# First sweep of a hybrid encoder layer: projection weights in another column order, with another row pitch, and small tiles at the end of their pool

## The chip, the core and the metric

The kernel runs on one core of one Trainium2 chip. The metric is the device time of one execution in microseconds (us), taken as the median of several runs. Beside the timed runs there is one profiled execution, whose page and trace give the start and the duration of every instruction. Engines are named as the profile does: PE (TensorE, matmul), PEld (its weight loads), DVE (VectorE), ACT (ScalarE), POOL (GpSimd), SP (the queue that issues most transfers).

## The reference

One encoder layer on x of shape (1, 2048, 1024), float32. One combined input projection feeds two mixers, whose outputs are joined, projected and added to the residual before a layer norm:

```python
h = x @ w_in
(g_q, g_k, g_v, g_gate, g_lr_f, g_lr_b,
 m_cq, m_ckv, m_kr, m_gate) = jnp.split(h, idx, axis=-1)
o_a = gla_branch(g_q, g_k, g_v, g_gate, g_lr_f, g_lr_b, wg2_f, bg_f, wg2_b, bg_b, gla_norm_g)
o_b = mla_branch(m_cq, m_ckv, m_kr, m_gate, positions, q_norm_g, w_uq, kv_norm_g, w_ukv)
mixed = jnp.concatenate([o_a, o_b], axis=-1) @ w_out
x = layer_norm(DEEPNORM_ALPHA * x + mixed, ln_g[layer], ln_b[layer])
```

Mixer A is gated linear attention with 4 heads (key width 64, value width 128), computed in chunks, as a forward and a backward scan that are summed. Mixer B is latent attention with 4 heads and a dense softmax over all 2048 keys.

## The kernel before

Every matmul operand is a float32 number split into a high and a low part (both of type float32r), and every product is three matmuls into one PSUM tile: high x high, high x low, low x high (`mm3`, lines 418 to 422; in the profile L420, L421 and L422). In `mm3(out, ah, al, bh, bl)` a is the stationary operand, which is loaded anew for each matmul, and b the moving one.

The work is done in four stages. The first sweep (`sweep_a`, some 22 to 350 us after the weights have come) walks the 16 chunks of 128 rows of x from the last to the first. For a chunk it computes the projections for mixer A's low-rank decay, q, k and v: the transposed chunk of x (tiles `xah` and `xal`, 8 blocks of 128 x 128) is stationary, and the weight rows `wah{k}` and `wal{k}` (k = 0 to 7, one tile of 128 x 1056 for each part) move, in three column groups of 288, 384 and 384 columns: `A_GROUPS = ((0, 288), (288, 384), (672, 384))`. Column group 0 holds the low-rank columns and q, group 1 k and the first head of v, group 2 the other three heads of v. The products of a group land in one PSUM tile `ipa` (`products`, lines 735 to 755). Between them stand, in a fixed order per chunk, the small products of the scan: transposes `qT`, `kT`, `kt`, `lrT`, the decay product `z`, the scores inside a chunk `Ap` (`ga_intra`), the output `Op` (`ga_av`) and the state update `Up` (`ga_state`). A fourth group `ipg` computes a gate of 512 columns with other weights (`wgh`, `wgl`).

The second sweep (`sweep_c`, to some 600 us) does the projections and the small products of mixer B (`ipm`, `pz`, `pq`, `pqr`) and combines the scan's state (`Sf`, `SU`, `MMb`, `qhb`, `qlb`, product `Ob`); then come the attention (`pS`, `o`) and the output projection (`po`, `pmb`, `px`).

The order of instructions on each engine is written out (`STEPS_A`, `ORDER_A` and tables of places), so that an edit of a tile's address alone does not reorder the first sweep. Tiles live in pools, which place them one behind the other in a partition. The pool `wa` holds the first sweep's weights and fixed tiles; behind it stand, first, the staging tiles `was` for the weights as they come from memory and later the pool `g1` with the working tiles of a chunk. So the size of a small tile early in `wa` shifts all that comes after it. The tiles of the second sweep are laid over this region, and their first writers wait until the earlier tiles that they overlap have had their last reader. SP issues its transfers in program order: a transfer that waits holds back those behind it.

The lines that the change touches:

```python
wa = [[wp.tile([P, NA], F32R, name=f"wa{p}{k}") for p in "hl"] for k in range(NK)]
...
self.mm3(pt[:, :n], xh[:, k, 0], xl[:, k, 0], wh[:, c0:c0 + n], wl[:, c0:c0 + n],
         start=(k == 0), stop=(k == NK - 1))
```

Of the kernel before, what the change touches and what calls it, by code (L numbers as in the profile page):

```python
# [9 lines left out]
F32 = mybir.dt.float32  # L10
F32R = mybir.dt.float32r
# [7 lines left out]
P = 128  # L19
S = 2048  # L20
D = 1024
NK = D // P
NCH = S // P
H = 4
NA = 1056
W_PIECES = ((2, 2, 2, 2), (2, 2, 2, 2), (2, 2, 2, 2))
A_GROUPS = ((0, 288), (288, 384), (672, 384))
QB = 512
NQB = S // QB
NKT = S // P  # L30
# [114 lines left out]
    xh=(-0.19, -0.054),  # L145
# [27 lines left out]
    xl=(-0.154, 0.109),  # L173
# [51 lines left out]
    xh=(-0.3, 1.403),  # L225
# [27 lines left out]
    xl=(1.031, 1.013),  # L253
# [37 lines left out]
    xh=(-0.262, -0.109),  # L291
# [27 lines left out]
    xl=(-0.244, 0.038),  # L319
# [36 lines left out]
class K:  # L356
# [254 lines left out]
    def sweep_a(self):  # L611
        tc, nc, ins, cp = self.tc, self.nc, self.ins, self.cp
        with ExitStack() as ctx:
            wp = ctx.enter_context(tc.tile_pool(name="wa", bufs=1, reuse_waits="tile"))
            xp, ip, tr, gp = self.xab, self.ip, self.tr, self.gp


            wa = [[wp.tile([P, NA], F32R, name=f"wa{p}{k}") for p in "hl"] for k in range(NK)]
            mask = wp.tile([P, P], I32, name="mask")
            rmask = wp.tile([P, H, P], F32, name="rmask")  # L620
            wgm = wp.tile([98, 1], F32, name="wgm")
            wg = wp.tile([98, H, P], F32R, name="wg")
            lrs = [wp.tile([P, 98], F32R, name=f"lr{i}") for i in range(2)]
            qbh = [wp.tile([P, H, 2, P], F32R, name=f"qbh{i}") for i in range(1)]
            qbl = [wp.tile([P, H, 2, P], F32R, name=f"qbl{i}") for i in range(1)]
            Sb = wp.tile([P, H, P], F32, name="Sb")
            pos_i = wp.tile([P, NCH], I32, name="pos_i")
            pos_f = wp.tile([P, NCH], F32, name="pos_f")
            invf = wp.tile([P, 32], F32, name="invf")
            hpi = wp.tile([P, 1], F32, name="hpi")  # L630
            self.cos = self.keep.tile([P, NCH, 32], F32, tag="rm", name="cos")
            self.sin = self.keep.tile([P, NCH, 2, 32], F32, tag="acc", name="sin")
            nc.scalar.preload_act_table_set(EXP_LN)
            for t in lrs:
                nc.vector.memset(t[:, 96:98].bitcast(F32), 1.0)
            for t in qbh + qbl:
                nc.gpsimd.memset(t.bitcast(F32), 0.0)
            nc.vector.memset(Sb, 0.0)

            with tc.tile_pool(name="sta", bufs=1, reuse_waits="tile") as sta:  # L640
                xf = self.load_x(NCH - 1, "xa", 1, 2)
                xcur = self.split_x(xp, xf, NCH - 1, "xa", "dve", 2)
                wgf = sta.tile([98, H * P], F32, name="wgf")
                wgh = sta.tile([98, H * P], F32R, name="wgh")
                W, wdone = wa, []
                for g, (c0, n) in enumerate(A_GROUPS):
                    k = 0
                    for m in W_PIECES[g]:
                        st = sta.tile([P, m, n], F32, name=f"was{g}_{k}")
                        nc.sync.dma_start(st, ins["wA"][k:k + m, :, c0:c0 + n].rearrange("k p n -> p k n"))  # L650
                        for e in range(m):
                            wh, wl = wa[k + e]
                            ops = (self.hi(wh[:, c0:c0 + n], st[:, e]),
                                   self.lo(wl[:, c0:c0 + n], st[:, e], wh[:, c0:c0 + n]))
                        k += m
                        wdone.append(ops)
                    if g == 0:
                        nc.sync.dma_start(self.ident, ins["ident"])
                        nc.sync.dma_start(wgf, ins["wg"])
                        nc.sync.dma_start(wgm, ins["wgm"])  # L660
                xnext = self.split_x(xp, self.load_x(NCH - 2, "xa", 1, 2), NCH - 2, "xa", "dve", 2)
                nc.sync.dma_start(rmask, ins["rmask"])
                nc.sync.dma_start(mask, ins["mask"])
                self.hi(wgh, wgf)
                nc.vector.scalar_tensor_tensor(wg.rearrange("p h d -> p (h d)"), wgh.bitcast(F32), wgm[:, 0:1],
                                               wgf, ALU.mult, ALU.add)
            nc.sync.dma_start(pos_i, ins["pos"])
            nc.sync.dma_start(invf, ins["invf"])
            g1 = ctx.enter_context(tc.tile_pool(name="g1", bufs=1))

            cst = dict(qbh=qbh[0], qbl=qbl[0], Sb=Sb, mask=mask, rmask=rmask, wg=wg, g1=g1, tr=tr, gp=gp)
            rope = self.rope_angles(pos_i, pos_f, invf, hpi)
            ch = self.ch = [dict(cst, c=NCH - 1 - i, i=i, lr=lrs[i % 2]) for i in range(NCH)]
            self.wa = wa
            run = lambda n, i: [0 for _ in getattr(self, "ga_" + n)(ch[i])]
            ch[0]["x"], ch[1]["x"] = xcur, xnext

            def step(i, steps):

                def after(g, k):  # L680
                    for n, d in steps.get((g, k), ()):
                        run(n, i if d == "cur" else i - 1)
                for g in range(3):
                    for k in self.products(ch[i], g, after):
                        pass
                    after(g, NK - 1)
                if i and ch[i]["c"] not in LATE_GATES:
                    for k in self.gate_products(ch[i]["c"], *ch[i]["x"], ip):
                        after(3, k)
                    self.gate_end(ch[i]["c"], g1)  # L690

            self.first_lr = wdone[7][0]
            step(0, {(1, 7): [("lrT", "cur")]})
            run("bst", 0)
            self.wgr = [self.wgp.tile([P, 512], F32, tag="wg", name=f"wgr{k}") for k in range(NK)]
            for k, raw in enumerate(self.wgr):
                nc.sync.dma_start(raw, ins["wB"][k, :, 0:512])
            self.wgh = [self.wgp.tile([P, 512], F32R, tag="wg", name=f"wgh{k}") for k in range(NK)]
            gens, last = {}, {}
            for t in ORDER_A.split():  # L700
                n, i = t.split(".")
                if t not in gens:
                    gens[t] = getattr(self, "ga_" + n)(int(i) if n in ("wg", "ld", "x") else ch[int(i)])
                with self.in_order(last):
                    next(gens[t], None)
            for n, g in gens.items():
                assert not list(g), n
            for i in range(4, NCH):
                c = ch[i]["c"]
                if c > 0:  # L710
                    for f in (self.ga_ld, self.ga_x):
                        for _ in f(i + 1):
                            pass
                else:
                    self.xlate = [self.split_x(xp, self.load_x(NCH - 1, "xb"), NCH - 1, "xb")]
                    self.xraw = self.load_x(NCH - 2, "xb")
                step(i, STEPS_A)
                if i < 4 + 5:
                    with self.after(ch[i]["zdone"]):
                        next(rope)  # L720
                if i == 9:
                    self.rope_tables(hpi)
            i = NCH - 1
            run("q", i)
            run("k", i)
            run("av", i - 1)
            for k in self.gate_products(0, *ch[i]["x"], ip):
                if k == 5:
                    run("kt", i)
                    run("intra", i)  # L730
            self.gate_end(0, g1)
            run("state", i)
            run("av", i)

    def products(self, d, g, after=lambda g, k: None):

        nc, c, i, g1 = self.nc, d["c"], d["i"], d["g1"]
        c0, n = A_GROUPS[g]
        xh, xl = d["x"]
        if i == 0 and g == 2:  # L740
            pt = self.gp.tile([P, 1024], F32, tag="gp", name=f"ipa{c}_{g}")
# [1 line left out]
            pt = self.ip.tile([P, 512], F32, tag="ip", name=f"ipa{c}_{g}")  # L743
        d["pt", g] = pt
        for k in range(NK):
            wh, wl = self.wa[k]
            self.mm3(pt[:, :n], xh[:, k, 0], xl[:, k, 0], wh[:, c0:c0 + n], wl[:, c0:c0 + n],
                     start=(k == 0), stop=(k == NK - 1))
            if k < NK - 1:
                after(g, k)  # L750
            yield k
# [145 lines left out]
    def ga_sums(self, d):  # L897
# [7 lines left out]
        V.tensor_tensor_scan(f2(b)[64:128, ::-1], f2(rmask)[64:128, ::-1], f2(za)[64:128, ::-1],  # L905
                             0.0, ALU.mult, ALU.add)
        yield
        cl = d["cl"] = d["g1"].tile([P, 3, H], F32, tag="cl", name=f"cl{c}")
        V.tensor_copy(cl[0:64, 0], b[0:64, :, 63])
        V.tensor_copy(cl[64:128, 0], b[64:128, :, 64])  # L910
        V.tensor_copy(cl[0:64, 2], b[0:64, :, 127])
# [1100 lines left out]
```

## Time and profile before

| | before |
|---|---|
| median of 3 runs | 1317.59 us (1316.13 to 1318.52) |
| span of the profiled execution | 1311.9 us |
| median less that span (no separate time of the profiled execution is given) | 5.7 us |
| TensorE busy | 1288.3 us, 98% |
| VectorE, ScalarE, GpSimd busy | 958.5, 812.5, 784.6 us |
| mean granted TensorE clock | 0.998 |

In a row of a group the profile gives line, engine, operation, out<-in by the program's names (buffer numbers left out), the shapes, how often it occurs, then the busy time in us, the mean ns of one instruction, and the idle time of the engine just before them with what ended it. Matmuls are pipelined: the duration of one includes a part that overlaps the next one.

### The profile page before, as it was taken

How to read it: one execution, taken by the hardware profiler on the slowest of the kernel's cores; microseconds unless marked ns; L12 is line 12 of the kernel's file. 1: busy time of each engine (PE TensorE's matmuls, PEld its weight loads, DVE VectorE, ACT ScalarE, POOL GpSimd, SP SyncE). 2: the span in 40 equal slices, each digit the busy share in tenths (PEclk: the TensorE clock that was granted, in tenths of full speed). 3: DMA queues.
4: the chain of work that ended last, by engine and by line, in shares of the span. 5: the costliest groups of instructions: out<-in, count | busy, mean ns of one | idle time of the engine just before them, and what ended most of it. 6: DMA issues, size and time to landing. Idle time of an engine off the chain costs nothing.

```text
span 1311.9 us, 19981 instructions
## 1 busy us (share of the span) xinstructions
PE 1288.3 (98%) x7081; PEld 1129.9 (86%) x7081; DVE 958.5 (73%) x1712; ACT 812.5 (62%) x1339; POOL 784.6 (60%) x494
## 2 busy tenths in 40 slices
PE   7999999999999999999999999999999999999997
PEld 7999999999989999999788888888888887888786
DVE  7967684655675455554888888888888888468998
ACT  6765656555575656564687787888888888511110
POOL 0143333232457666671388888889999999844441
PEclk9999999999999999999999999999999999999999
DMA  8131313122475555565301111112223210366663
GB/s 283 61 100 53 93 53 92 49 76 71 147 245 173 197 194 177 201 202 177 121 1 41 41 42 41 41 57 59 63 66 102 51 41 9 121 208 174 210 195 121
DMA packets 107819, 145.81 MB, mean 111 GB/s; under 512 B 17250, under 2 KB 62694, under 8 KB 107720
## 3 DMA queue, kind: packets, MB, share of 16 engines
q1 hardware_dynamic: 99128, 142.41, 35.0%
q0 software_dynamic: 672, 2.10, 0.4%
q8 instruction: 56, 0.92, 0.3%
q10 hardware_dynamic: 7920, 0.03, 0.3%
q14 instruction: 43, 0.35, 0.2%
HBM read 94.14 MB, written 50.36 MB: 110 GB/s over the span
## 4 chain that ended last, share of the span: by engine, by line
PE 83%; DVE 4%; DMA 3%; ACT 2%; issue 2%; POOL 1%; SPq 1%; DVEq 0%; POOLq 0%; ACTq 0%
PE o L420 4%; PE o L421 4%; PE pS L1521 4%; PE pS L1524 4%; PE o L422 4%; PE pS L1523 4%; PE pS L1525 4%; PE pS L1522 4%; PE ipa L420 4%; PE ipa L422 4%; PE ipa L421 4%; PE pz L421 2%; PE pz L420 2%; PE pz L422 2%; PE ipg L420 2%; PE ipg L421 2%
## 5 line engine op out<-in xcount | busy, mean ns | idle before, releaser
L372 POOL TENSOR_TENSOR pl<-s,ph 128x1024 fp32r<-128x1024 f32 x128 | 306.9, 2412 | 66.7 <-ACT ph L366 61.5
L1543 DVE TENSOR_TENSOR rm<-pS,rm 128x512 f32<-128x512 f32 x210 | 144.8, 690 | 44.1 <-ACT s L1530 39.0
L1530 ACT ACTIVATE s<-pS 128x1024 f32<-128x1024 f32 x128 | 131.2, 1025 | 67.6 <-PE pS L1525 65.6
L1567 DVE TENSOR_TENSOR s<-s,mb 128x1024 f32<-128x1024 f32 x128 | 151.2, 1213 | 9.5 <-PE mb L1561 9.3
L1030 POOL TENSOR_TENSOR Us<-Us,cw 128x512 f32<-128x512 f32 x16 | 18.5, 1157 | 227.0 <-DVE Us L1028 175.2
L366 ACT ACTIVATE ph<-s 128x1024 fp32r<-128x1024 f32 x128 | 135.0, 1057 | 18.1 <-PE o L422 17.6
L1571 ACT ACTIVATE s<-s 128x1024 f32<-128x1024 f32 x128 | 131.4, 1050 | 13.8 <-DVE s L1567 13.7
L420 PE MATMUL ipa<-wah,xah 128*128 128x384 f32 (+1 forms) x384 | 130.6, 340 | 6.8 <-ACT wah L366 6.8
L422 PE MATMUL ipa<-wah,xal 128*128 128x384 f32 (+1 forms) x384 | 125.2, 326 | 0.0
L421 PE MATMUL ipa<-wal,xah 128*128 128x384 f32 (+1 forms) x384 | 125.0, 325 | 0.0
L1521 PE MATMUL pS<-qh,ckvT_h 128*128 128x512 f32 x256 | 103.7, 405 | 0.7 <-ACT s L1571 0.4
L420 PE MATMUL o<-ph,vh 128*128 128x512 f32 x256 | 102.6, 401 | 0.0
L422 PE MATMUL o<-ph,vl 128*128 128x512 f32 x256 | 101.3, 396 | 0.0
L1524 PE MATMUL pS<-rh,krs 128*128 128x512 f32 x256 | 101.2, 395 | 0.0
L421 PE MATMUL o<-pl,vh 128*128 128x512 f32 x256 | 101.1, 395 | 0.0
L1523 PE MATMUL pS<-qh,ckvT_l 128*128 128x512 f32 x256 | 100.9, 394 | 0.0
L1525 PE MATMUL pS<-rl,krs 128*128 128x512 f32 x256 | 100.7, 393 | 0.0
L1522 PE MATMUL pS<-ql,ckvT_h 128*128 128x512 f32 x256 | 100.6, 393 | 0.0
L1594 DVE TENSOR_TENSOR ap<-ap,s 128x512 f32<-128x512 f32 x120 | 83.1, 693 | 2.7 <-ACT s L1571 0.8
L372 POOL TENSOR_TENSOR ol<-of,oh 128x512 fp32r<-128x512 f32 x32 | 43.0, 1346 | 65.6 <-ACT oh L366 65.6
L420 PEld LDWEIGHTS ipa<-wah,xah 128*128 128x128 f32 x384 | 73.5, 192 | 7.6 <-ACT wah L366 6.8
L420 PE MATMUL pz<-xch,wzh 128*128 128x256 f32 x256 | 74.8, 292 | 0.0
(325 smaller groups left out, 3856.4 us busy)
## 6 DMA issues: line engine op xcount, KB each, us to landing
xcf<-xT_dram SPq DMA_DIRECT2D x16, 512.0 KB, 4.7
xr<-x_dram SPq DMA_DIRECT2D x16, 512.0 KB, 6.5
out_dram<-rr SPq DMA_DIRECT2D x32, 256.0 KB, 2.0
xaf<-xT_dram SPq DMA_DIRECT2D x14, 512.0 KB, 4.2
oib<-oi_s SPq DMA_DIRECT2D x16, 256.0 KB, 4.1
qdb<-qd_s SPq DMA_DIRECT2D x16, 256.0 KB, 4.6
SU<-su_s SPq DMA_DIRECT2D x16, 256.0 KB, 4.4
ub<-u_s SPq DMA_DIRECT2D x16, 256.0 KB, 4.7
```

Source lines behind the costliest of these rows:

```text
L366: return nc.scalar.activation(dst, src, AF.Copy).ins
L372: return e.tensor_tensor(dst, src, hi.bitcast(F32), ALU.subtract).ins
L420: mm(out, ah, bh, start=start, stop=False)
L421: mm(out, ah, bl, start=False, stop=False)
L422: mm(out, al, bh, start=False, stop=stop)
L1521: mm(ps[:, e], kh, qh, start=True, stop=False)
L1522: mm(ps[:, e], kh, ql, start=False, stop=False)
L1523: mm(ps[:, e], kl, qh, start=False, stop=False)
L1524: mm(ps[:, e], kr, rh, start=False, stop=False)
L1525: mm(ps[:, e], kr, rl, start=False, stop=True)
L1543: V.tensor_tensor(d["rm"], src[:, e], d["rm"], ALU.max)
L1567: V.tensor_tensor(s, s, d["mb"][:, None, :].to_broadcast([P, 2, QB]), ALU.subtract)
```

## The change

The weight tiles of the first sweep get a row pitch of 1088 columns in place of 1056, and the three column groups change places inside the tile: `A_HOME` puts group 1 at column 0, group 2 at 384 and group 0 at 768. `A_GROUPS` still says which columns of the weights in memory belong to a group, so the transfers and the shapes of all instructions stay as they are. In the pool the small tiles (`wgm`, the two `lr`) go behind the large ones, the tile `cl` moves from the pool `g1` into `wa` as one fixed tile, and a tile `fill` of 80 columns is added that nothing reads or writes.

The byte address in a partition, modulo 256, of the first sweep's operands:

| tile | before | after |
|---|---|---|
| `wah` rows, at column 0 | 192 | 192 |
| `wal` rows, at column 0 | 64 | 192 |
| group 0 (288 columns), high and low part | 192, 64 | 192, 192 |
| groups 1 and 2 (384 columns), high and low part | 64, 192 | 192, 192 |
| `xah`, `xal` (stationary) | 192 | 192 |
| `qbh`, `qbl`, `Sb` | 32 | 192 |
| `wg` | 224 | 192 |
| working tiles in `g1`, staging tiles `was` | 64 or 128 | 192 |

```diff
+A_HOME = (768, 0, 384)
+WA_PITCH = 1088
...
-            wa = [[wp.tile([P, NA], F32R, name=f"wa{p}{k}") for p in "hl"] for k in range(NK)]
+            wa = [[wp.tile([P, WA_PITCH], F32R, name=f"wa{p}{k}") for p in "hl"] for k in range(NK)]
             mask = wp.tile([P, P], I32, name="mask")
             rmask = wp.tile([P, H, P], F32, name="rmask")
-            wgm = wp.tile([98, 1], F32, name="wgm")
             wg = wp.tile([98, H, P], F32R, name="wg")
-            lrs = [wp.tile([P, 98], F32R, name=f"lr{i}") for i in range(2)]
...
             Sb = wp.tile([P, H, P], F32, name="Sb")
+            wgm = wp.tile([98, 1], F32, name="wgm")
+            lrs = [wp.tile([P, 98], F32R, name=f"lr{i}") for i in range(2)]
...
+            self.cl = [wp.tile([P, 3, H], F32, name=f"cl{i}") for i in range(1)]
+            wp.tile([P, 80], F32, name="fill")
...
-                            wh, wl = wa[k + e]
-                            ops = (self.hi(wh[:, c0:c0 + n], st[:, e]),
-                                   self.lo(wl[:, c0:c0 + n], st[:, e], wh[:, c0:c0 + n]))
+                            wh, wl = (t[:, A_HOME[g]:A_HOME[g] + n] for t in wa[k + e])
+                            ops = self.hi(wh, st[:, e]), self.lo(wl, st[:, e], wh)
...
-        c0, n = A_GROUPS[g]
+        c0, n = A_HOME[g], A_GROUPS[g][1]
...
-            wh, wl = self.wa[k]
-            self.mm3(pt[:, :n], xh[:, k, 0], xl[:, k, 0], wh[:, c0:c0 + n], wl[:, c0:c0 + n],
+            wh, wl = (t[:, c0:c0 + n] for t in self.wa[k])
+            self.mm3(pt[:, :n], xh[:, k, 0], xl[:, k, 0], wh, wl,
...
-        cl = d["cl"] = d["g1"].tile([P, 3, H], F32, tag="cl", name=f"cl{c}")
+        cl = d["cl"] = self.cl[0]
```

In the built program each engine's instructions up to the end of the first sweep are the same, in the same order, with the same waits. Where the second sweep begins, some first writers wait for other releases, because the tiles beneath them have moved.

## The prediction

> **What bounds the kernel now.** I read the page first, then the table of stages, then the groups of TensorE by shape in the stage that the change touches, then the chain of starts and waits where the first sweep hands over to the next.
>
> ```profile
> span 1311.9 us, 19981 instructions
> PE 1288.3 (98%) x7081; PEld 1129.9 (86%) x7081; DVE 958.5 (73%) x1712; ACT 812.5 (62%) x1339; POOL 784.6 (60%) x494
> PEclk9999999999999999999999999999999999999999
> ```
>
> TensorE is busy in 98% of the span at the full granted clock, so time can only come from its own products or from the few places where it waits. The table of stages (columns: window, its length, busy us and instructions of each engine, clock, DMA share, GB/s) shows where those places are.
>
> ```profile
> 0.00:22.00 22.00, 15.10 (x73) 14.10 (x73) 14.86 (x32) 15.37 (x33) 2.04 (x6) 1.00 0.93 296
> 22.00:350.00 328.00, 325.97 (x2066) 307.86 (x2067) 216.81 (x385) 194.50 (x388) 101.22 (x72) 1.00 0.27 79
> 350.00:600.00 250.00, 246.51 (x1724) 233.51 (x1722) 145.72 (x464) 155.17 (x389) 161.77 (x164) 1.00 0.59 195
> ```
>
> The first 22 us wait for weights from memory (DMA share 0.93); the change alters neither the transfers nor their order, so they stay. From 22 to 350 us, the first sweep, TensorE waits 2.0 us of 328: a faster VectorE or ScalarE instruction there buys next to nothing, a faster matmul buys all of its shortening. So the question is what the new addresses do to one matmul.
>
> **The matmuls and their byte residues.** As the built programs place the tiles (byte address in a partition, modulo 256), the stationary operands xah and xal lie at 192 in both kernels. The moving operands are the weights. Before, the rows of the high part start at 192 and those of the low part at 64 (row pitch 4224 bytes, 128 over a multiple of 256); column 0 keeps that, columns 288 and 672 add 128 more. So the 288-wide group has high 192, low 64, and the two 384-wide groups have high 64, low 192. After, all are at 192. The first sweep also moves its working tiles (64, 128 or 32 before) to 192. The groups by shape, 22 to 350 us:
>
> ```profile
> L420 PE MATMUL ipa<-wah,xah 128*128 128x384 f32 x240 | 84.6, 353 | 0.0
> L422 PE MATMUL ipa<-wah,xal 128*128 128x384 f32 x240 | 81.0, 338 | 0.0
> L421 PE MATMUL ipa<-wal,xah 128*128 128x384 f32 x240 | 80.4, 335 | 0.0
> L420 PE MATMUL ipg<-wgh,xah 128*128 128x512 f32 x104 | 41.2, 396 | 0.0
> L421 PE MATMUL ipg<-wgl,xah 128*128 128x512 f32 x104 | 40.6, 391 | 0.0
> ...
> L420 PE MATMUL ipa<-wah,xah 128*128 128x288 f32 x120 | 36.7, 306 | 0.1
> L421 PE MATMUL ipa<-wal,xah 128*128 128x288 f32 x120 | 35.3, 294 | 0.0
> L422 PE MATMUL ipa<-wah,xal 128*128 128x288 f32 x120 | 35.3, 294 | 0.0
> ```
>
> The last number before the second bar is the mean ns of one, which includes the drain that overlaps the next matmul; differences between rows of one shape are differences in pace. Over the whole run there are 256 of each 384-wide form and 128 of each 288-wide one. In the 384-wide rows, the one whose moving operand already lies at 192 (L421, low weights) is the shortest, 335 ns, and the two at 64 take 338 and 353.
>
> **Part 1, the 384-wide products.** Upper bound of the gain: L422 comes down to L421's 335, which is 3 ns x 256 = 0.8 us. L420 is first in every group of three and has a surplus of its own: in the gate product ipg, where everything lies at 192 already, L420 takes 5 ns more than L421. So it could come down from 353 to 340: 13 ns x 256 = 3.3 us. Together 4.1 us. Lower bound: nothing. The 288-wide rows speak for it, since there L421 at 64 and L422 at 192 both take 294 ns. A small loss is also thinkable (the rival below). I take half of the upper bound, 2.0 us: the 18 ns by which L420 stands over L421 is partly the restart after other products are put between, as the 288-wide L420 shows with 12 ns at residue 192.
>
> **Part 2, the small products of the sweep.** VV and the operands beside it go from 64 and 128 to 192. They come in pairs of 256 and 128 columns (Op and Up). The same pair stands in the second sweep as Ob, where both operands already share a residue (224). The wider ones over the whole run:
>
> ```profile
> L1418 PE MATMUL Ob<-MMb,qhb 128*128 128x256 f32 x64 | 16.4, 331 | 0.7 <-POOL MMb L372 0.4 <-DVE gm L1209 0.3
> L1004 PE MATMUL Op<-VV,Ah 128*128 128x256 f32 x64 | 15.8, 323 | 0.3 <-ACT Ah L366 0.3
> ```
>
> 331 ns at one residue, 323 at two: a common residue buys nothing here, and I cost this part at 0 (bounds: 8 ns x 128 = 1.0 us slower to nothing).
>
> **Part 3, VectorE, ScalarE, GpSimd and the new tiles.** The stream of instructions up to the end of the sweep is the same, with the same waits; the tile cl becomes one fixed tile in place of a pool's single buffer, which keeps the same order of writer and reader; the filler is never touched. Whatever the addresses do to these engines is covered by TensorE in a stage where they are busy at most 217 us of 328. Cost 0. If that cover went, each of some 25 VectorE instructions in a chunk could matter, but a wait of 2.0 us in the whole stage leaves it far.
>
> **Part 4, the hand-over.** The second sweep's first tiles overlie the first sweep's, and since those moved, some loads wait for other releases. In the order of the built program, the load wkr (the SP queue) waited for GpSimd's Us and the store of it (su_s); after the change it waits for a VectorE subtraction (Al) that ends at 362.8, and the load wqT behind it takes over the wait for su_s. In order of time, with the wait of SP for that store (total, times, longest) as the last line:
>
> ```profile
> 362.14 0.68 DVE L372 TENSOR_TENSOR Al<-At,Ah 128x512 fp32r<-128x512 f32 x1
> ...
> 364.37 0.33 SPq L1369 DMA_DIRECT2D oib<-oi_s  x1
> ...
> 365.74 0.38 SPq L1141 DMA_DIRECT2D gkv_b<-gkv_bc_dram  x1
> 369.60 0.33 SPq L1141 DMA_DIRECT2D wkr<-wqr_dram  x1
> 369.98 0.42 SPq L1141 DMA_DIRECT2D wkr<-wkT_dram  x1
> 370.50 1.22 SPq L1141 DMA_DIRECT2D wqT<-wqT_dram  x1
> ...
> 372.98 0.84 SPq L1369 DMA_DIRECT2D SU<-su_s  x2
> SPq L1141 <- DMA su_s<-Us: 3.3, 1, 3.3
> ```
>
> What hangs on it, in order of time (in brackets the idle time before an instruction and what ended it):
>
> ```profile
> 378.48 1.66 POOL L1390 TENSOR_TENSOR Sf<-Sf,SU 64x512 f32<-64x512 f32 x1 [5.37 <-DMA SU<-su_s]
> 382.38 0.61 ACT L366 ACTIVATE MMb<-SU 128x512 fp32r<-128x512 f32 x1
> 385.56 1.27 POOL L372 TENSOR_TENSOR qlb<-qdb,qhb 128x512 fp32r<-128x512 f32 x1
> 386.88 0.33 PE L1419 MATMUL Ob<-MMb,qlb 128*128 128x128 f32 x1 [0.85 <-POOL qlb L372]
> ```
>
> wkr's two loads then go out right behind gkv_b, near 366.1, and wqT at 369.6 in place of 370.5, so SU follows 0.9 us earlier. GpSimd waits 5.4 us for SU at 378.48 and from there works almost without a pause to qlb, for which TensorE waits 0.85 us. With SU 0.9 us earlier that wait is about gone: a gain of 0.85 us, lower bound 0 (if the landing does not follow the issue). What is late next: of GpSimd's steps before qlb, MMb needs its high part from ScalarE, which is there at 383.0, well ahead of GpSimd. Two other moved waits:
>
> ```profile
> 360.75 0.22 PE L1023 MATMUL Up<-VV,ktl 128*128 128x128 f32 x1
> 371.41 0.48 DVE L1102 MEMSET Sf<- 64x512 f32 x1
> 356.79 0.55 POOL L938 DMA_DIRECT2D qd_s<-qd  x1
> ```
>
> The load oib, and SP's queue behind it, gets a wait for the last of Up, which is done at 361.0, 3.4 us before oib is issued. The memset of Sf, and VectorE's queue behind it, gets a wait for the store of qd, issued 14.6 us before the memset starts. Both stay at 0.
>
> **Sum.** 2.0 + 0.85 = 2.85 us from the span of 1311.9, so 1309.0; with the 5.7 us between that span and the median (1317.59) as they are, 1314.7. No more than 0.2% (2.6 us) either way is about what a measurement of this kernel can tell from no change, so the forecast lies just past that line.
>
> **Rivals.** *Residues cost nothing.* For it: the equal 294s and the Ob pair. Then only the hand-over is left: 1317.59 - 0.85 = 1316.7, and 1317.6 if that too is hidden. The Trainium skill says as much in TensorE: Matmul & The Clock Gate, Part 2 (What happens when you issue a matmul): TensorE has two independent read ports on SBUF, so loading the next weights takes nothing from the running matmul; by it the two streams could not collide at any residue. The 294s agree with it, the 335 against 353 does not settle it.
>
> *Residues matter in all of the sweep.* Attention's eight 512-wide groups, whose operands differ in residue, take more than ipg's 391:
>
> ```profile
> L421 PE MATMUL o<-pl,vh 128*128 128x512 f32 x256 | 101.1, 395 | 0.0
> ```
>
> Were those 4 ns the residue's price on each of 1152 projection products, 4.6 us would go, with the hand-over 5.5: 1312.1. Against it: other engines are much busier in attention.
>
> *Slower: one residue is the worse one.* If the stream of columns and the next weights, marching from the same residue, meet in the same part of SBUF, each product pays. For it, two groups of 256 columns in the second sweep: pz has both operands at 192, pq has 224 against 192.
>
> ```profile
> L421 PE MATMUL pz<-xcl,wzh 128*128 128x256 f32 x256 | 72.8, 285 | 0.0
> ...
> L421 PE MATMUL pq<-cqT_l,wabs_h 128*128 128x256 f32 x64 | 17.8, 278 | 0.0
> ```
>
> 7 ns apart. On the 1152 projection products and 192 of Ap: 4 ns each, about half, gives 5.4 us, less 0.85, so +4.5: 1322.1. It decides from 2.6 ns per product, where 3.5 - 0.85 passes 0.2%. Against it: 335 at residue 192 is the shortest of its shape.
>
> **Chances.** Forecast case 0.45, of it 0.35 past 0.2% and 0.10 short of it; residues in all of the sweep 0.12; nothing 0.20; slower 0.23, of it 0.02 too small to be told. So faster 0.47, same 0.32, slower 0.21. The forecast's own range is 1312.6 (both upper bounds, 4.1 + 0.85) to 1316.7 (the hand-over alone). The wide range goes past the larger gain's 1312.1 to 1311.5, takes in all of "nothing", and reaches into the slower case to 1321.5; it leaves out about 0.05 below and 0.13 above.
>
> **What would show it.** Right: in the first sweep L420 and L422 of the 384-wide shape near 345 and 335, the 288-wide rows unchanged, chunks (of some 22 us) shorter by 0.1 us each, SU issued near 372.1 and no wait of TensorE before Ob. Wrong: 353 and 338 as before (nothing), or 288-wide rows over 294 and L421 over 335 (slower); or a difference that grows after 400 us, where no address has changed.

## The result: 1319.2 us, some 3 us slower

Forecast were 1314.7 us and "faster"; measured were 1319.2 us (1315.35 to 1321.37, 22 runs) against 1315.8 us (1313.8 to 1319.31, 22 runs) of the kernel before. The ratio is 1.0021, with a 95% interval of 1.0014 to 1.0029: 2.8 us slower, 1.8 to 3.8 (the two medians by themselves differ by 3.4 us). The direction was wrong. That the time lies inside the wide range is luck: the range reached so far up for the rival that one residue is the worse one, and that is not what happened. The forecast was also counted from 1317.59, the median of three runs; from the 1315.8 of 22 runs, its gain of 2.85 us would have given 1313.0.

### The profile after

The change adds two or three lines to the file, so L420 to L422 are now L422 to L424, L372 is L374, L1418 is L1421. First the page's span and busy times, then the table of stages, with a narrow row around the hand-over that the prediction did not cut out.

```profile
span 1316.8 us, 19977 instructions
PE 1290.1 (98%) x7081; PEld 1129.7 (86%) x7081; DVE 961.0 (73%) x1712; ACT 813.4 (62%) x1339; POOL 784.8 (60%) x494
```

```profile
22.00:350.00 328.00, 326.65 (x2072) 308.29 (x2072) 216.87 (x386) 194.53 (x388) 101.10 (x72) 1.00 0.26 78
350.00:380.00 30.00, 29.21 (x159) 25.09 (x158) 25.19 (x33) 20.71 (x36) 14.28 (x16) 1.00 0.91 306
380.00:395.00 15.00, 12.65 (x94) 11.55 (x93) 8.57 (x20) 10.50 (x27) 10.14 (x11) 1.00 0.40 112
```

And the last of these windows in the kernel before:

```profile
380.00:395.00 15.00, 14.15 (x115) 13.87 (x114) 7.49 (x23) 9.34 (x27) 14.76 (x16) 1.00 0.56 172
```

The first sweep is as full as it was (TensorE works 326.65 of 328 us, before 325.97). Between 380 and 395 us TensorE works 1.5 us less, at the full clock. VectorE and ScalarE work about 1.1 us longer there and GpSimd 4.6 us less. Something is late at the hand-over.

The groups of the first sweep by shape (22 to 350 us; the last number before the bar's end is the mean ns of one, as before):

```profile
L422 PE MATMUL ipa<-wah,xah 128*128 128x384 f32 x240 | 84.3, 351 | 0.0
L423 PE MATMUL ipa<-wal,xah 128*128 128x384 f32 x240 | 80.7, 336 | 0.0
L424 PE MATMUL ipa<-wah,xal 128*128 128x384 f32 x240 | 80.6, 336 | 0.0
L422 PE MATMUL ipa<-wah,xah 128*128 128x288 f32 x120 | 36.6, 305 | 0.0
L424 PE MATMUL ipa<-wah,xal 128*128 128x288 f32 x120 | 35.3, 294 | 0.0
L423 PE MATMUL ipa<-wal,xah 128*128 128x288 f32 x120 | 35.3, 294 | 0.0
```

353, 335, 338 (L420, L421, L422) became 351, 336, 336. Of the 13 and 3 ns of the upper bound, 2 and 2 appear, L421 lost one, and all this is only in the durations, which overlap. What counts is the distance from the start of one product to the start of the next. Worked out from the starts of the recorded products, its mean was 182.6 ns (group 1) and 178.4 ns (group 2) before, and is 182.6 and 178.5 ns now. Inside a set of three it shifted a little: in group 2, the distances behind the first, second and third product were 186.4, 172.3 and 175.5 ns, and are 185.1, 175.1 and 174.1. What one product gained the next gave back. The sweep gained nothing.

Where the time went is read from when each matmul starts, counted from the span's start, in this kernel less in the kernel before. I call that the lag. It is -0.69 us at 22 us (a start that differs from execution to execution), and -0.55 us at 350 us. Then it jumps, between 381 and 388 us, to +1.95 us. The hand-over, in order of time:

```profile
365.73 0.44 SPq L1144 DMA_DIRECT2D wkr<-wqr_dram  x1
366.21 0.48 SPq L1144 DMA_DIRECT2D wkr<-wkT_dram  x1
368.52 0.33 SPq L1144 DMA_DIRECT2D wqT<-wqT_dram  x1
...
370.00 0.86 SPq L1372 DMA_DIRECT2D SU<-su_s  x2
SPq L1144 <- DMA su_s<-Us: 1.7, 1, 1.7
```

wkr goes out right behind gkv_b, as forecast. SU leaves SP at 370.0, 3.0 us earlier than before; forecast were 0.9. The missing part: the store su_s that SP waits for (last line: 1.7 us) was there 1.1 us earlier, and wqT's issue took 0.33 us in place of 1.22. (This execution was 0.55 us ahead by 350 us, which is part of these 1.1 us. It makes the leads named below larger, and the delays smaller, by as much.) What this releases (POOL, then VectorE's eight wzl subtractions as one block, here and in the kernel before, then ScalarE, GpSimd, TensorE):

```profile
375.16 1.34 POOL L1393 TENSOR_TENSOR Sf<-Sf,SU 64x512 f32<-64x512 f32 x1 [2.70 <-DMA SU<-su_s]
376.57 1.37 POOL L1398 TENSOR_TENSOR SU<-Sf,cw 64x512 f32<-64x512 f32 x1
378.02 1.37 POOL L1390 TENSOR_TENSOR Sf<-Sf,cw 64x512 f32<-64x512 f32 x1
379.47 1.62 POOL L1393 TENSOR_TENSOR Sf<-Sf,SU 64x512 f32<-64x512 f32 x1
...
374.07 8.96 DVE L374 TENSOR_TENSOR wzl<-wzr,wzh 128x512 fp32r<-128x512 f32 x8
...
378.53 0.63 ACT L368 ACTIVATE wzh<-wzr 128x512 fp32r<-128x512 f32 x1 [2.51 <-DVE wzl L374]
381.67 0.63 ACT L368 ACTIVATE wzh<-wzr 128x512 fp32r<-128x512 f32 x1 [2.51 <-DVE wzl L374]
383.08 0.19 PEld L424 LDWEIGHTS pz<-xch,wzl 128*128 128x128 f32 x1 [0.37 <-DVE wzl L374]
385.31 0.32 POOL L1298 TENSOR_TENSOR krf<-krf,rope 128x64 f32<-128x64 f32 x1 [4.23 <-DVE rope L1473]
385.58 0.62 ACT L368 ACTIVATE MMb<-SU 128x512 fp32r<-128x512 f32 x1
386.27 1.26 POOL L374 TENSOR_TENSOR MMb<-SU,MMb 128x512 fp32r<-128x512 f32 x1 [0.64 <-ACT MMb L368]
387.49 1.27 POOL L374 TENSOR_TENSOR qlb<-qdb,qhb 128x512 fp32r<-128x512 f32 x1
...
387.59 0.39 PE L1421 MATMUL Ob<-MMb,qhb 128*128 128x256 f32 x1 [1.25 <-POOL MMb L374]
388.81 0.33 PE L1422 MATMUL Ob<-MMb,qlb 128*128 128x128 f32 x1 [0.84 <-POOL qlb L374]
```

The same block in the kernel before:

```profile
374.71 5.97 DVE L372 TENSOR_TENSOR wzl<-wzr,wzh 128x512 fp32r<-128x512 f32 x8
```

GpSimd's four steps on the state, which used to start at 378.48, as the wzl block was ending, now start at 375.16 and run in the middle of it. The block takes 8.96 us in place of 5.97. The durations in the view by tile (minimum, median, maximum of the eight, in ns), before and after:

```profile
L372 DVE TENSOR_TENSOR wzl<-wzr,wzh x8: 675/678/1593, 374.7 to 379.1; 128x512 fp32r<-128x512 f32 x8
```

```profile
L374 DVE TENSOR_TENSOR wzl<-wzr,wzh x8: 674/1108/1777, 374.1 to 382.3; 128x512 fp32r<-128x512 f32 x8
```

Before, one of eight is slow; after, four are, at 1.5 to 1.8 us instead of 0.68. Each of the four starts (at 375.27, 376.97, 378.42, 379.87) 0.1 to 0.4 us after one of GpSimd's steps does, and ends 0.55 us after that step has ended. The rest follows: ScalarE's wzh waits for wzl, 2.51 us twice; MMb's high part, behind it on ScalarE, starts at 385.58 in place of 382.38; GpSimd waits 4.23 us for rope, a step of VectorE behind the block, and 0.64 us more for MMb's high part; MMb's low part and qlb are 2 us late, and TensorE waits 1.25 + 0.84 us at Ob where it had waited 0.85. Ahead of that, three of its weight loads for pz wait for wzl itself (0.29, 0.19 and 0.37 us). So 1.0 of the 2.5 us appears at pz and 1.5 at Ob; MMb sets the sum, since it is complete 1.94 us later than before (387.53 in place of 385.59) in an execution that was 0.55 us ahead.

### The profile page after: what moved, and what is told of

Same layout as the page of the kernel before. It is cut to its first block, busy times and chain, and to the rows that moved or that the text cites. A ratio compares the mean times of both kernels' runs of the same rounds, so it can differ in the third digit from the quotient of the medians.

```text
span 1316.8 us, 19977 instructions
## 1 busy us (share of the span) xinstructions
PE 1290.1 (98%) x7081; PEld 1129.7 (86%) x7081; DVE 961.0 (73%) x1712; ACT 813.4 (62%) x1339; POOL 784.8 (60%) x494
## 4 chain that ended last, share of the span: by engine, by line
PE 54%; DVE 6%; DMA 4%; issue 2%; POOL 2%; ACT 2%; SPq 1%; DVEq 0%; POOLq 0%; ACTq 0%
PE o L422 4%; PE o L423 4%; PE pS L1524 4%; PE o L424 4%; PE pS L1527 4%; PE pS L1526 4%; PE pS L1528 4%; PE pS L1525 4%; DMA xr<-x_dram 2%; PE pz L423 2%; PE pz L424 2%; PE pz L422 2%; DVE rr L1945 1%; PE ipm L424 1%; PE ipm L422 1%
## 5 line engine op out<-in xcount | busy, mean ns | idle before, releaser
L374 POOL TENSOR_TENSOR pl<-s,ph 128x1024 fp32r<-128x1024 f32 x128 | 307.0, 2413 | 67.1 <-ACT ph L368 61.9
L368 ACT ACTIVATE ph<-s 128x1024 fp32r<-128x1024 f32 x128 | 135.0, 1056 | 18.2 <-PE o L424 17.7
L422 PE MATMUL ipa<-wah,xah 128*128 128x384 f32 (+1 forms) x384 | 130.1, 339 | 5.8 <-ACT wah L368 5.8
L424 PE MATMUL ipa<-wah,xal 128*128 128x384 f32 (+1 forms) x384 | 124.6, 324 | 0.0
L422 PE MATMUL o<-ph,vh 128*128 128x512 f32 x256 | 102.6, 401 | 0.0
L424 PE MATMUL o<-ph,vl 128*128 128x512 f32 x256 | 101.3, 396 | 0.0
L374 POOL TENSOR_TENSOR ol<-of,oh 128x512 fp32r<-128x512 f32 x32 | 43.0, 1344 | 67.9 <-ACT oh L368 67.9
L422 PEld LDWEIGHTS ipa<-wah,xah 128*128 128x128 f32 x384 | 73.4, 191 | 6.9 <-ACT wah L368 6.1
L422 PE MATMUL pz<-xch,wzh 128*128 128x256 f32 x256 | 74.8, 292 | 0.0
```

What stands on the lines that cost most here:

```text
L368: return nc.scalar.activation(dst, src, AF.Copy).ins
L374: return e.tensor_tensor(dst, src, hi.bitcast(F32), ALU.subtract).ins
L422: mm(out, ah, bh, start=start, stop=False)
L424: mm(out, al, bh, start=False, stop=stop)
```

## The experiments

My theory after this: the residues are worth nothing, and the loss is the earlier SU, which lets GpSimd's steps slow VectorE's subtractions. The rivals: the new addresses cost something of their own, in the sweep or in the second sweep's first tiles; or the early transfer itself, and not GpSimd's work, disturbs VectorE.

| kernel | lag at 22 us | 22 to 350 | 350 to 391 | 391 to 600 | 600 to 1210 | 1210 to 1285 |
|---|---|---|---|---|---|---|
| after | -0.69 | +0.14 | **+2.50** | +0.67 | +0.04 | +1.37 |
| e1 after, SU late | +0.06 | +0.25 | **-0.31** | +0.17 | -0.04 | +2.46 |
| e2 before, SU early | +0.66 | -0.05 | **+2.06** | +0.06 | -0.02 | +3.08 |
| e3 after again | +0.32 | +0.18 | **+4.01** | +0.13 | -0.02 | +1.48 |
| e4 after, Sf behind | -0.97 | +0.13 | **+0.61** | +1.44 | +0.12 | +2.70 |
| e5 before, Sf behind | +0.25 | -0.04 | **+0.72** | +2.50 | -0.02 | +1.39 |
| e6 after, residues mixed | -0.15 | +1.22 | **+3.97** | +0.15 | +0.02 | +3.14 |
| e7 before again | -0.18 | -0.06 | **+0.01** | +0.07 | +0.10 | +2.75 |
| e8 before, qlb on VectorE | -0.29 | -0.04 | **-1.03** | -0.02 | 0.00 | +0.84 |
| e9 after, SU late, qlb on VectorE | -1.24 | +0.20 | **-1.02** | +0.03 | 0.00 | +0.63 |
| e10 after, other residues | -1.20 | -0.47 | **+2.54** | +0.10 | -0.05 | +3.28 |
| e11 as e8 | -0.68 | +0.01 | **-0.96** | +0.02 | +0.02 | +0.26 |
| e12 as e9 | -0.21 | +0.28 | **-1.03** | +0.01 | +0.02 | +0.80 |

Each row is one profile: lag against the first profile of the kernel before at 22 us, and then what is added to it in each stretch (us from the span's start, as in the kernel before), in us, worked out from the starts of the same matmuls. The first and the last column differ between executions of one kernel (e7 is the kernel before, unchanged), so what the change did stands in the four columns between. The 0.67 us of the first profile after from 391 to 600 us did not come again in e3, e6 or e10 (0.10 to 0.15).

### e1: the changed kernel with a late SU

```diff
-    u15=-0.21,
+    u15=-0.65,
...
-    lS=(-1.12, -1.093),
+    lS=(-0.64, -0.63),
```

The numbers are places in the written order: u15 that of the store of ub, lS those of SU's two loads, which now follow it.

> The changed kernel, with SU's two loads issued later on SP, behind the store of ub (u_s15), so that they land some 3 to 4 us later, about when they landed before the change. Theory (GpSimd's steps on SU, released early, hold up VectorE's eight subtractions wzl): seven of the eight wzl take 0.68 us again, TensorE's wait before Ob shrinks from 2.5 us to 1.2 us or less, and the time falls by about 2 us, to within 0.1% of the kernel before. Rival (the new addresses, or the moved waits in front of MMb and qlb, cost the time): wzl and Ob as in the changed kernel, no more than 0.5 us gained.

Ratio 1.0008 (0.9999 to 1.0016) beside 1.0034 for the changed kernel (e3). SU was issued at 375.5, GpSimd's steps began at 378.47, and the addresses were those of the change:

```profile
L374 DVE TENSOR_TENSOR wzl<-wzr,wzh x8: 678/681/1754, 375.0 to 380.4; 128x512 fp32r<-128x512 f32 x8
386.86 0.33 PE L1422 MATMUL Ob<-MMb,qlb 128*128 128x128 f32 x1 [0.53 <-POOL qlb L374]
```

Two subtractions are slow (1754 and 1357 ns) where four had been; I had expected one. TensorE's wait for MMb is gone, and 0.53 us for qlb is left. The 2.5 us at the hand-over are the timing of SU, not an address.

### e2: the kernel before with an early SU

```diff
-    lS=(-1.12, -1.093),
+    lS=(-1.4, -1.39),
```

> The kernel before, all its addresses kept, with SU's two loads issued ahead of gq, gkv_b, wkr and wqT on SP. Theory: SU lands near 374 us in place of 378.5, three or four of the eight wzl take 1.5 to 1.8 us, Ob starts some 2 us later, and the time grows by 1.5 to 3 us. Rival (addresses or moved waits): nothing of that, the time stays within 0.5 us.

Ratio 1.0024 (1.0015 to 1.0034): the kernel before, with SU's two loads moved and no address changed, is as slow as the changed one. Four subtractions are slow (1.2 to 1.7 us).

```profile
L372 DVE TENSOR_TENSOR wzl<-wzr,wzh x8: 679/939/1745, 375.3 to 383.0; 128x512 fp32r<-128x512 f32 x8
388.31 0.39 PE L1418 MATMUL Ob<-MMb,qhb 128*128 128x256 f32 x1 [0.22 <-POOL MMb L372]
PE pabs L1165 <- DMA wqT<-wqT_dram: 1.3, 1, 1.3
```

It is not a clean copy. SU now stands ahead of wqT on SP, and TensorE waits 1.3 us for wqT first (last line, from the waits), which is where most of its 2.06 us appears. But that does not set the end: when Ob's turn comes, MMb is still the later one, and behind it stand the same waits as in the changed kernel (ScalarE's wzh for wzl, 5.0 us in all).

### e3: the changed kernel again

> The changed kernel once more, for a second profile. The slow wzl and TensorE's wait before Ob (2.5 us) must come back if they are caused by the order of the instructions. Of the two other places where the first profile of the changed kernel lost time (0.4 us at pz near 527 us, 1.4 us at pmb near 1217 us) I expect at least the second to be of another size, because it waits for transfers.

Ratio 1.0034 (1.0021 to 1.0047). The slow subtractions are those of the first profile (677/1107/1776 ns, 5.6 us of waits on ScalarE), yet the hand-over cost 4.0 us in place of 2.5. The table of stages shows why:

```profile
380.00:395.00 15.00, 12.65 (x81) 11.47 (x81) 8.68 (x18) 9.45 (x24) 10.06 (x11) 0.89 0.35 103
```

The granted clock (the number behind the busy times) is 0.89 here, 1.00 in the first profile: after the same two waits at Ob the products ran at about half pace for some 3.3 us (an estimate: 0.11 of 15 us, twice), and 448-wide ones started every 0.37 us in place of 0.20. So the stall has a second price, some 1.5 us, that is not paid in every execution: e3 and e6 paid it, the first profile and e10 didn't. These four profiles with the early SU and the new addresses lost 2.5, 4.0, 4.0 and 2.5 us at the hand-over, 3.25 on average, which lies within the measured 1.8 to 3.8 us.

The Trainium skill, page TensorE: Matmul & The Clock Gate, Part 1, has the array at half clock after an idle window of about 3.4 us. The half pace agrees; the length doesn't quite, since two waits of 1.26 and 0.84 us sufficed here and in other executions did not.

### e4 and e5: GpSimd's second pair of steps behind MMb and qlb

The same edit in the changed kernel (e4) and in the kernel before (e5):

```diff
-    Sf1=(-1.303, -0.348),
-    Sf2=(-0.613, -0.339),
+    Sf1=(-1.303, 0.03),
+    Sf2=(-0.613, 0.035),
```

> The changed kernel, with GpSimd's two steps for the next chunk's state (Sf times cw, Sf plus SU) put behind MMb and qlb of the first chunk. Theory: two of the four slow wzl are 0.68 us again, ScalarE's wzh come 2 us earlier, TensorE's wait before Ob falls by about 2 us, and the time falls by 1.5 to 2.5 us against the changed kernel. Rival (addresses or moved waits): less than 0.5 us.

> The kernel before, with one edit: the second half of GpSimd's steps on the next chunk's state (the writers of Sf) is placed behind its two splits of the hand-over (MMb and qlb) instead of ahead of them. If the hand-over is set by GpSimd's queue (my theory), MMb and qlb come early, TensorE's wait of 0.85 us ahead of Ob goes, and the one slow wzl subtraction (1593 ns) is near 680 ns. In the changed kernel the same move brought the hand-over's 2.4 us back but not the time, since GpSimd's xcl came 0.9 us later to the second ipm group; so I expect here 0.8 us won at Ob, 0.9 us lost at that group, and a ratio of 0.999 to 1.002. The rival, that GpSimd's order is worth its wait, expects 0.999 or less: no wait at the later group.

e4 leaves SU as early as in the changed kernel (issued at 369.8) and only takes two of GpSimd's four steps out from under the block:

```profile
L374 DVE TENSOR_TENSOR wzl<-wzr,wzh x8: 674/680/1782, 373.8 to 380.1; 128x512 fp32r<-128x512 f32 x8
PE ipm L424 <- POOL xcl L374: 1.3, 1, 1.3
```

Two subtractions are slow (1782 and 1523 ns), as expected, and the hand-over costs 0.6 us in place of 2.5. So it isn't the early transfer that slows VectorE, it is GpSimd's instructions. All fourteen profiles say the same: of their 112 wzl, the 38 that took 1.19 us or more started while one of GpSimd's steps ran and ended 0.55 us after it, and the 74 that took 0.67 to 0.69 us started while none ran. But the time hardly came back: ratio 1.0023 (1.0014 to 1.0031), a median of 1 us below e3's where I had expected 1.5 to 2.5, and the two intervals overlap. The postponed steps hold back GpSimd's xcl, and TensorE waits 1.3 us for it at 402 us (0.4 before), as e4's second line shows. In e5 the same wait appears. Its ratio is 0.9995 (0.9986 to 1.0004), inside what was expected, but the profile shows neither the quick block nor the 0.8 us won at Ob: GpSimd's first step began at 376.99 in place of 378.48, two subtractions were slow (1781 and 1521 ns), and TensorE waited 0.5 and 0.8 us at Ob. After the wait for xcl the granted clock was 0.89 from 395 to 410 us, which is part of the 2.50 us in its row. That profiled execution was the slowest of its eleven, so the row is not the typical one. Neither run shows a faster kernel by this order.

### e6 and e10: the groups at different residues

> The changed kernel, with the home of the weight columns moved so that the three groups' operands no longer start at one byte residue modulo 256 (64, 236 and 24 bytes; pitch and order as changed). If residues are inert (my theory), the first sweep from 22 to 350 us runs at the changed kernel's pace: the 384-wide groups at 335 to 352 ns, no lag over 0.4 us gained or lost between 22 and 380 us, and the time is that of the changed kernel, some 3 us above the kernel before (ratio 1.001 to 1.004). If one residue is worth what the prediction said (2.0 us, or 4 ns for each 384-wide product), this kernel loses it again: 2 us of lag, evenly over the sweep. If the new residue was the worse one, it gains up to 4 us.

```diff
-A_HOME = (768, 0, 384)
+A_HOME = (800, 11, 406)
```

> The changed kernel with the three groups at byte residues 64, 0 and 0 modulo 256 instead of 192 throughout: mixed as in the sixth experiment, but every group starts at a multiple of 64 bytes. There the first sweep from 22 to 350 us grew by 1.2 us, evenly, where six kernels with multiples of 64 stayed within 0.3 us. If what counted was that 236 and 24 are no multiples of 64, this one grows by no more than 0.3 us between 22 and 350 us. If one common residue is worth 1 us after all, and the kernel before (64 and 192) was only lucky, it grows by 1 us again. The hand-over at 375 to 390 us is as slow as in the changed kernel in either case.

```diff
-A_HOME = (768, 0, 384)
+A_HOME = (800, 16, 400)
```

e6 ran at a ratio of 1.0025 (1.0011 to 1.0038), the changed kernel's, but its sweep grew by 1.2 us, evenly, against my expectation of at most 0.4. e10 answers whether that was the lost common residue: its groups lie at 64, 0 and 0, none at the 192 of the stationary operand, and its sweep is the shortest of all, 0.5 us below the kernel before. I had expected a growth, of 0.3 us at most or of 1 us. Its hand-over is as slow as in the changed kernel, as expected; it was timed once (1318.15 us), so it has no ratio.

```profile
L422 PE MATMUL ipa<-wah,xah 128*128 128x384 f32 x240 | 83.9, 349 | 0.0
L424 PE MATMUL ipa<-wah,xal 128*128 128x384 f32 x240 | 80.6, 336 | 0.0
L423 PE MATMUL ipa<-wal,xah 128*128 128x384 f32 x240 | 80.6, 336 | 0.0
```

Addresses do seem to matter, then, by about 2 ns a product: between starts, group 2 takes 180.6 ns at residue 24, 178.4 to 178.6 with 64 and 192 or with 192 alone, and 176.7 at 0; group 1 takes 180.3 at 236 and 180.2 at 0, and 182.2 to 182.6 otherwise. That is no effect of one common residue, and multiples of 64 alone don't explain group 1 either. Six profiles with all operands at 192 grew by 0.13 to 0.28 us over the sweep, five of the old placement by -0.06 to +0.01: the change costs the sweep 0.2 us. What rule stands behind the 2 ns stays open; e6's sweep and e10's rest on one profile each.

### e7: the kernel before again

> The kernel before, unchanged, for a second profile and the scatter of the comparison. All theories: ratio 1.000 within 0.001. The profile tells which of the small spots belong to the execution and which to the kernel: TensorE's wait ahead of pmb8 at 1216 us was 0.9 us in the first profile of this kernel and 1.8 to 2.4 us in the five others. If that is the loads' scatter, it will be near 2 us here, and then 1.1 to 1.5 us of the difference between the first two profiles isn't the change's; if it follows from the shifted hand-over, it will be near 0.9 us again. The waits of 0.85 us ahead of Ob and the one slow wzl of 1.6 us come again in any case.

Ratio 0.9992 (0.9981 to 1.0003). The middle columns repeat within 0.1 us. The waits at Ob and the one slow wzl (1585 ns) came again, as expected. Not so the output projection at 1216 us, where TensorE waits for a residual sum that waits for loads. First profile, then e7:

```profile
1216.51 0.47 PE L420 MATMUL pmb<-woh,oh 128*128 128x512 f32 x1 [0.94 <-DVE rr L1927]
```

```profile
1217.61 0.47 PE L420 MATMUL pmb<-woh,oh 128*128 128x512 f32 x1 [2.10 <-DVE rr L1927]
1218.60 0.63 PE L420 MATMUL pmb<-woh,oh 128*128 128x512 f32 x1
1219.03 0.63 PE L421 MATMUL pmb<-wol,oh 128*128 128x512 f32 x1
```

After the longer wait products start every 0.43 us in place of 0.23, at a granted clock of 0.66 from 1217 to 1222 us in place of 1.00. This spot cost 2.75 us more in e7 than in the first profile of the same kernel. So the 1.37 us that the changed kernel shows there is scatter, and comparing two single spans (1316.8 - 1311.9 = 4.9 us) would have overstated the change.

### e8, e9, e11, e12: the last input taken off GpSimd

The kernel before (e8, e11) and the changed kernel with the late SU (e9, e12), with the first chunk's qlb on VectorE:

```diff
-        self.lo(d["ql"], d["qdb"], d["qh"], "pool")
+        self.lo(d["ql"], d["qdb"], d["qh"], "pool" if d["st"] or d["c"] else "dve")
```

> The kernel before, with one edit: the first chunk's qlb subtraction (1.27 us on GpSimd, issued at 385.56 and the last input that TensorE waits for at Ob) is done by VectorE, behind its first wabs product. If GpSimd's queue sets the hand-over (my theory), Ob's wait of 0.84 us for qlb goes (qlb done by 385 us at the latest, MMb at 385.59 as before), the later products start 0.8 us earlier, and xcl's wait of 0.4 us shrinks; ratio 0.9985 to 1.000. The rival, that another input of the hand-over is as late and takes its place, expects the same time within 0.3 us and a new wait of 0.5 us or more ahead of Ob or within the next 15 us.

> The changed kernel with the state's load SU issued later (as in the first experiment, where it came within 0.001 of the kernel before) and with the first chunk's qlb on VectorE as well. If the new addresses do nothing and the loss was all in the hand-over, this runs like the kernel before with that one edit: same ratio within 0.001, the same waits ahead of Ob within 0.1 us. If the addresses bring something of their own, the two differ by it: 2 us in the first sweep by the prediction.

> The kernel before with the first chunk's qlb on VectorE, once more, since the profile showed 1.05 us won at Ob but the ratio of 0.9996 [0.9986, 1.0006] could not tell it from none. If the 1.05 us last to the end: 0.9992 again within the interval, 0.9985 to 1.000. If something later takes them back, 1.000 and a profile whose lead of 1 us at 391 us is gone by the end.

> The changed kernel with the late load SU and the first chunk's qlb on VectorE, once more, for the same reason: the same ratio as the run beside it within 0.001, and the same pace of the first sweep within 0.3 us, since the new addresses bring nothing.

In all four profiles the wait ahead of Ob is gone and 1.0 us is won between 350 and 391 us, which lasts to 1210 us. In e8:

```profile
383.53 0.68 DVE L372 TENSOR_TENSOR qlb<-qdb,qhb 128x512 fp32r<-128x512 f32 x1
385.40 0.38 PE L1418 MATMUL Ob<-MMb,qhb 128*128 128x256 f32 x1
385.63 0.22 PE L1419 MATMUL Ob<-MMb,qlb 128*128 128x128 f32 x1
```

This shows the 0.85 us of the prediction's part 4 to be real, and GpSimd's queue to set it. The time hardly shows it: 0.9996 (0.9986 to 1.0006) and 0.9996 (0.9987 to 1.0005), then 0.9999 (0.9991 to 1.0008) and 1.0002 (0.9993 to 1.0011). All four beat the changed kernel (their intervals end at 1.0011 or below, where its own begins at 1.0014); that any beats the kernel before is not shown. Old and new addresses, e8 beside e9 and e11 beside e12, agree within 0.0003. In e8 and e11 three wzl are slow, since GpSimd's steps began at 377.26 and 376.47 there, and neither pz nor Ob waited for them: slow subtractions need not cost time. In e9 qlb met two of GpSimd's steps (Sf, and MMb's low part):

```profile
381.92 2.84 DVE L374 TENSOR_TENSOR qlb<-qdb,qhb 128x512 fp32r<-128x512 f32 x1
```

That is 2.84 us for a subtraction that takes 0.68 in e8; e12 repeats it with 2.83.

## Why the prediction was wrong

**Part 1, the 384-wide products, -2.0 us.** This term was mis-sized: it measured +0.2 us for the whole sweep. The lower bound, nothing, was right, and the equal 294s of the 288-wide rows that spoke for it were the better witness. I read 353 and 338 against 335 as a price of the residue. They are durations that overlap; the mean distance between starts was the same before and after, and the first product of a set of three still has the longest (186.4 and 185.1 ns in group 2). Had I taken the distances from the trace of before, group 2, at residues 64 and 192, would have stood at 178.4 ns and group 1, at the same residues, at 182.6: a difference that no residue explains.

**Parts 2 and 3, nothing.** Right as far as the sweep goes: it holds all of them, and changed by 0.2 us.

**Part 4, the hand-over, -0.85 us.** This is the step that failed. The first half held: wkr no longer waits and SU comes earlier, even by 3.0 us where I had 0.9. The sentence that failed is "What is late next", where I said that MMb's high part was on ScalarE by 383.0, "well ahead of GpSimd". That time was taken from the trace of before and kept, as though ScalarE and VectorE did not feel that GpSimd's steps move. They do: moved by 3.3 us, the steps fell on the wzl block, wzl made wzh wait, and MMb's high part was done at 386.2. The term's size was off too, since I had SU 0.9 us earlier and not 3.0. In place of 0.85 us won, 2.5 us were lost, and 1.5 more where the clock fell.

The trace of before had the sign of it. One of the eight wzl took 1593 ns against 678, the one that started at 379.09, under GpSimd's step of 378.48. I passed over the maximum in that row. The Trainium skill, page SBUF — State Buffer, section SBUF: two separate sides, states the mechanism: VectorE and GpSimd share one pair of ports, which is locked for the length of an instruction, and a VectorE operation with two inputs in SBUF is kept out while GpSimd reads there. The runs agree: 0.68 us alone, 1.2 to 1.8 under one step, with the end always 0.55 us after that of the step, and 2.84 under two.

**The rivals.** "Residues cost nothing" was right about the sweep, and its 1316.7 wrong by the same hand-over. "Residues matter in all of the sweep" is refuted by the unchanged mean spacing. "One residue is the worse one" had the right sign of the result for the wrong reason: 0.2 us of 5.4. Of the tests that were named, "a difference that grows after 400 us" came near; the place was 381 to 388 us, and my list of what would show it asked only whether the wait ahead of Ob went, not what it would turn into.

## What to carry to other kernels

When an edit lets one engine's work start earlier, lay its instructions at their new times over those of the other engines, before taking a gain; the times that the others had are not theirs to keep. VectorE's two-input operations and GpSimd's steps are the pair to look at first, and a maximum of 1593 beside a median of 678 in one row already says that they meet. And compare the starts of pipelined matmuls, not their durations, before pricing anything by a few ns.

## What the hardware showed that I had not expected

- A VectorE subtraction of 128 x 512 in float32 took 0.68 us alone, 1.2 to 1.8 us when it started under one GpSimd step on 64 x 512, and 2.84 us under two; so four GpSimd steps of 1.34 to 1.62 us lengthened a block of eight from 5.97 us (one of them slow) to 8.96 us.
- Waits of TensorE of about 2 us cost more than themselves in some executions: the granted clock fell to 0.89 over 15 us (e3, e6) or 0.66 over 5 us (e7), and products then started every 0.43 us in place of 0.23 (e7). The same waits in the first profile after, and in e10, had no such cost.
- One common byte residue of operands modulo 256 is worth nothing that can be seen in 1344 products (0.2 us lost); other column offsets moved the mean distance between starts by about 2 ns either way (e6, e10, one profile each).
